# Rotated q and k channel-major by DMA, and the causal mask by VectorE, in a two-layer hybrid decoder trunk

## The chip, the cores and the metric

The kernel runs on one core of one Trainium2 chip. A core has engines that each work through their own queue of instructions in order: TensorE (PE, matrix products from SBUF into PSUM), VectorE (DVE), ScalarE (ACT), GpSimd (POOL) and SyncE (SP, here only a queue that issues DMAs). They wait for each other by semaphores. The metric is the device time of one execution in microseconds (us).

## The reference

Two layers over 512 tokens with 1024 channels; everything is float32. Each layer normalises x, projects it into ten groups of 512 columns, runs four mixers, gates each and projects back. Cut to what the change touches:

```python
x += W_out( concat_g[ mixer_g(RMSNorm(x)) * silu(gate_g) ] )    # g = A: S5, B: differential attention,
                                                                 #     C: RG-LRU, M: attention to 256 memory tokens
def rope_partial(x, cos, sin):          # q and k, the first 16 of the 64 channels of each half head
    x1, x2, xp = xf[..., :half], xf[..., half:ROPE_DIMS], xf[..., ROPE_DIMS:]
    out = jnp.concatenate([x1 * cos - x2 * sin, x2 * cos + x1 * sin, xp], axis=-1)

def diff_attention(q, k, v, lam):       # 4 heads, two softmaxes each
    mask = kpos[None, :] <= qpos[:, None]
    s1 = jnp.where(mask, s1, -1e30)     # s1 = q1 k1^T / 8, s2 likewise
    p = jax.nn.softmax(s1, axis=-1) - lam * jax.nn.softmax(s2, axis=-1)
```

## The kernel before

**Numbers.** A float32 product is made of three fp32r products: each operand is split into hi (rounded by ACT) and lo (the rest, by DVE), and PE sums hi x hi, hi x lo and lo x hi in PSUM.

**Weights.** All weights come in 136 pieces of 128x1024. `w_load` (L148) brings a piece into one of two raw buffers by a DMA of SP's queue; `w_use` splits it: ACT casts `whi` (L166), DVE subtracts `wlo` (L172). There are three buffers of each, so ACT and DVE can be about three pieces ahead of PE. A piece gives PE 24 products of 512 columns.

**Blocks.** `ORDER` (L31) lists the projection blocks of a layer: q, k, v, kv (the memory keys mk and values mv), cx (the RG-LRU's input), au (S5's input), the gates ag, bg, cg, mg, the memory query mq, S5's gl, and the output blocks o. `cm_block` (L504) keeps weights stationary and writes channel-major (channels on partitions, tokens along the row; products L517); `tm_block` (L524) keeps the tokens stationary and writes token-major (L537). Both take accumulators from a PSUM pool of four (`acc`). After every 12 products a block yields, which is one tick.

**Streams.** The mixers are generators that advance between ticks (`Streams`, L59; `run`, L1116): attention, RG-LRU (`lru`), S5 (`s5`), memory attention, parameter set-up (`par`). What a generator yields is the number of ticks until it goes on (`D_AT` = 2 for the attention). A scheduler of the framework then fixes the order of the instructions on each engine; at run time every engine keeps to that order.

**q and k.** Both are projected token-major. `qk_evac` (L574) copies a token tile by ACT into `qz`, rotates 16 of each 64 channels with four small DVE operations (`rab`, `qz`), and two ticks later `flush_qk` (L591) transposes it with four PE transposes (L597) into channel-major. For q ACT copies the result (L600); for k ACT casts one half (L605) and DVE subtracts for the other, which makes `kT`, hi and lo in the two halves of the partitions. The attention starts when q, k and v are there (L1272).

**Attention** (L610) works through 16 items (four query tiles of 128 by four heads). An item has a score tile `sc` of two softmaxes from a PSUM pool with one buffer. PE writes the scores (L647, L648), then adds the mask with a product of a bf16 identity and a bf16 mask, one for each softmax (L650). DVE takes the maximum (L652), ACT the exponentials with their sums (L658), DVE combines the two softmaxes (L664); then PE transposes (L672), ACT copies `pT`, PE multiplies with v (L682), ACT scales the result and squares it (L683, L685).

**RG-LRU** (L724) starts after cx: PE makes the gates' products (L740 to L742), ACT evaluates tanh, exponentials and a square root (L743 to L756), DVE scans over the tokens (L760). `lru_load` (L1126) brings its weights through GpSimd's DMA queue, up to `BD_AHEAD` blocks ahead of cx. **S5** (L927) rotates, scans and turns back blocks of 512 columns on DVE, and moves small `MT` tiles by GpSimd's queue.

## Time and profile before

| | us |
|---|---|
| median of 3 runs (913.62 to 914.91) | 913.9 |
| the profiled execution | 913.18 |
| its span, first to last instruction | 911.4 |
| PE busy | 890.5 |
| DVE busy | 658.8 |
| ACT busy | 509.6 |
| GpSimd busy | 42.1 |

Busy time counts the time in which at least one instruction of the engine is under way. Instructions of one engine overlap at their ends, so the mean length of one is a little more than the distance at which they follow each other. A wait is given with the instruction that ended last before it (`<-`). The granted clock of TensorE was 1.00 of full speed in all stretches.

### The profile page before, as it was taken

What the parts mean: (1) busy time and instruction counts of PE and PEld (TensorE: products, weight loads), DVE (VectorE), ACT (ScalarE), POOL (GpSimd) and SP (SyncE); (2) the same over time, 40 slices, a digit from 0 to 9 for tenths busy, and PEclk for the clock granted to TensorE, in tenths of its full rate; (3) what the DMA queues carried; (4) which work ended last, traced back from release to release, by engine and by line L of the source; (5) the groups of instructions that cost most, each with busy time, mean ns of one, the idle gap of its engine ahead of it and who ended that gap; (6) DMA issues with size and microseconds to landing.
All of it is one profiled execution on the core that took longest, in us unless ns stands there. A gap on an engine that the chain in (4) does not pass through costs nothing.

```text
span 911.4 us, 12490 instructions
## 1 busy us (share of the span) xinstructions
PE 890.5 (98%) x4542; PEld 748.9 (82%) x4542; DVE 658.8 (72%) x1315; ACT 509.6 (56%) x1031; POOL 42.1 (5%) x86
## 2 busy tenths in 40 slices
PE   8999999999999999999999999999999999999996
PEld 5788888978878888888888888898888888788885
DVE  6985888678999856983474667764899996666343
ACT  6764887985434265922554568766655344863133
POOL 1001000001110100000100000000101110000000
PEclk9999999999999999999999999999999999999999
DMA  5733432212222237432343332432112222152322
GB/s 185 196 118 102 140 93 70 70 47 72 75 70 61 75 104 205 135 111 93 127 140 92 93 93 70 137 95 70 51 47 83 63 74 93 47 185 98 108 72 93
DMA packets 80930, 90.07 MB, mean 99 GB/s; under 512 B 23778, under 2 KB 58211, under 8 KB 80868
## 3 DMA queue, kind: packets, MB, share of 16 engines
q1 hardware_dynamic: 77842, 85.72, 30.3%
q10 hardware_dynamic: 722, 2.36, 0.8%
q0 software_dynamic: 2304, 1.18, 0.5%
q8 instruction: 36, 0.59, 0.3%
q14 instruction: 26, 0.21, 0.1%
HBM read 84.40 MB, written 4.19 MB: 97 GB/s over the span
## 4 chain that ended last, share of the span: by engine, by line
PE 72%; DVE 18%; ACT 6%; issue 2%; DMA 1%; SPq 0%; DVEq 0%; ACTq 0%
PE acc L537 37%; PE acc L517 17%; PE acc L1261 5%; DVE wlo L172 2%; DVE u L347 2%; DVE xr L1046 2%; DVE wt L347 2%; PE ms L682 1%; DVE xr L347 1%; PE tp L312 1%; PE sc L810 1%; PE tp L1012 1%; PE sc L647 1%; PE sc L648 1%; ACT whi L166 1%
## 5 line engine op out<-in xcount | busy, mean ns | idle before, releaser
L172 DVE TENSOR_TENSOR wlo<-raw,whi 128x1024 fp32r<-128x1024 f32 x136 | 166.2, 1222 | 125.3 <-ACT whi L166 121.6
L166 ACT CAST whi<-raw 128x1024 fp32r<-128x1024 f32 x136 | 143.1, 1052 | 194.1 <-PE acc L537 120.1
L517 PE MATMUL acc<-hThi,whi 128*128 128x512 f32 x384 | 154.3, 402 | 0.0
L517 PE MATMUL acc<-hThi,wlo 128*128 128x512 f32 x384 | 151.1, 394 | 0.0
L517 PE MATMUL acc<-hTlo,whi 128*128 128x512 f32 x384 | 150.6, 392 | 0.0
L537 PE MATMUL acc<-whi,hThi 128*128 128x512 f32 x256 | 104.1, 407 | 1.0 <-ACT whi L166 1.0
L537 PE MATMUL acc<-wlo,hThi 128*128 128x512 f32 x256 | 100.7, 393 | 0.0
L537 PE MATMUL acc<-whi,hTlo 128*128 128x512 f32 x256 | 100.7, 394 | 0.0
L537 PE MATMUL acc<-wlo,mxh 128*128 128x512 f32 x256 | 100.2, 391 | 0.0
L537 PE MATMUL acc<-whi,mxh 128*128 128x512 f32 x256 | 100.1, 391 | 0.0
L537 PE MATMUL acc<-whi,mxl 128*128 128x512 f32 x256 | 100.1, 391 | 0.0
L517 PEld LDWEIGHTS acc<-hThi,wlo 128*128 128x128 f32 x384 | 72.2, 188 | 15.0
L517 PEld LDWEIGHTS acc<-hTlo,whi 128*128 128x128 f32 x384 | 72.4, 189 | 13.4
L517 PEld LDWEIGHTS acc<-hThi,whi 128*128 128x128 f32 x384 | 72.4, 189 | 13.0
L537 PEld LDWEIGHTS acc<-whi,hThi 128*128 128x128 f32 x256 | 56.3, 220 | 9.1 <-ACT whi L166 1.4
L537 PEld LDWEIGHTS acc<-whi,hTlo 128*128 128x128 f32 x256 | 56.1, 219 | 7.8 <-DVE hTlo L315 0.2
L537 PEld LDWEIGHTS acc<-wlo,hThi 128*128 128x128 f32 x256 | 56.4, 220 | 7.1
L537 PEld LDWEIGHTS acc<-whi,mxl 128*128 128x128 f32 x256 | 48.1, 188 | 9.8
L537 PEld LDWEIGHTS acc<-wlo,mxh 128*128 128x128 f32 x256 | 48.1, 188 | 9.7
L537 PEld LDWEIGHTS acc<-whi,mxh 128*128 128x128 f32 x256 | 48.1, 188 | 9.6
L982 POOL DMA_DIRECT2D MT<-kq x64 | 32.1, 509 | 490.7 <-DVE kq L347 339.4
L658 ACT ACTIVATE e<-sc,nmx 128x128 f32<-128x128 f32 (+3 forms) x64 | 33.1, 524 | 7.1 <-DVE nmx L654 5.8
(316 smaller groups left out, 1642.2 us busy)
## 6 DMA issues: line engine op xcount, KB each, us to landing
raw<-in_w_in_dram SPq DMA_DIRECT2D x80, 512.0 KB, 3.7
raw<-in_w_out_dram SPq DMA_DIRECT2D x32, 512.0 KB, 3.3
raw<-in_w_mem_kv_dram SPq DMA_DIRECT2D x16, 512.0 KB, 3.3
...
```

Of the source, the lines that this page charges most:

```text
L166: S.copy(hi, wbuf[j])
L172: V.tensor_tensor(out=lo, in0=raw, in1=hi, op=ALU.subtract)
L312: lastins["pe"] = PE.transpose(pt[:, k, :], h[:, kk * 128:(kk + 1) * 128], ident)
L347: V.tensor_tensor(out=o, in0=a, in1=b, op=op)
L517: PE.matmul(a[j][:, :ncol], w[:, kk, c], h(k), start=(hf == 0 and i == 0), stop=(hf == 1 and i == 3 * nh - 1))
L537: PE.matmul(a[t], h(k, t), w[:, kk, :], start=(p == 0 and kk == 0 and i == 0), stop=(p == np_ - 1 and kk == 1 and i == 2))
L647: PE.matmul(s[:, m, :M], qh[:, m, h, :], kT[m][:, h, :M], start=True, stop=False)
L648: PE.matmul(s[:, m, :M], ql[:, m, h, :], kT[m][:, h, :M], start=False, stop=False)
L658: S.activation(e[:, m, :N], s[:, m, :N], AF.Exp, bias=nmx[:, m:m + 1], scale=0.125, accum_out=sm[:, m:m + 1])
L982: G.dma_start(out=MT[g * 64 + 64 - n:g * 64 + 64, g, t], in_=kq[g * 64:g * 64 + n])
L1046: V.tensor_tensor_scan(out=xr_[i][:, j, :], data0=dec, data1=xr_[i][:, j, :], initial=0.0, op0=ALU.mult, op1=ALU.add)
L1261: PE.matmul(a, w[:, k, s, j * 128:(j + 1) * 128], h[:, 2 * hf + k, :], start=(hf == 0 and i == 0), stop=(hf == 1 and i == 5))
```

## The change

- q and k are projected channel-major by `cm_block`; ACT copies each 128x512 block straight into `z` (`qz`, `kz`). No PE transposes.
- `rope` collects the 32 + 32 + 32 + 32 rotated rows of `z` by four DMAs of GpSimd's queue into `rx`, DVE does four operations with tables of cosines and sines, and four DMAs bring the rows back. For k four ACT casts and four DVE subtracts of 64x1024 then make `kT`. `D_ROPE` gives the ticks between these steps.
- The tables are built once in channel-major form (GpSimd copies `rep`, eight PE transposes, four ACT copies), kept in DRAM, and loaded again in layer 1.
- The mask is float32 in SBUF (`cmt`), and DVE adds it to the score tile in PSUM before the maximum; the products of L650 and the bf16 tiles are gone.
- v comes first in both layers; the attention starts after k, as soon as the rope is done; `BD_AHEAD` is 1.

```diff
-ORDER = ["q v k kv cx au cg bg mq ag mg gl oAM0 oAM1 oBC0 oBC1".split(),
-         "q k cx v kv au mq bg mg ag cg gl oAM0 oAM1 oBC0 oBC1".split()]
+ORDER = ["v q k kv cx au cg bg mq ag mg gl oAM0 oAM1 oBC0 oBC1".split(),
+         "v q k cx kv au mq bg mg ag cg gl oAM0 oAM1 oBC0 oBC1".split()]
...
-BD_AHEAD = 3
+BD_AHEAD = 1
...
+D_ROPE = {"q": ((2, 2), (2, 2)), "k": ((4, 4), (2, 2))}
...
+    rtab = [b2([P, L], f"rt{i}") for i in range(2)]
+    rtd = [dpool.tile([P, L], F32, tag=f"rtd{i}", name=f"rtd{i}") for i in range(2)]
+    for w, src in enumerate((rcos, rsin)):
+        rep_ = b2([P, NT, P], "rep")
+        for i in range(NT):
+            G.tensor_copy(rep_[:, i].rearrange("p (a f c) -> p a f c", a=4, c=4),
+                          src[:, i].unsqueeze(1).unsqueeze(3).to_broadcast([P, 4, 8, 4]))
+        pr = tp()
+        for i in range(NT):
+            PE.transpose(pr[:, i, :], rep_[:, i], ident)
+        pf = pr.rearrange("p i c -> p (i c)")
+        for s_ in range(2):
+            S.activation(rtab[w][s_ * 64:s_ * 64 + 64], pf[s_ * 64:s_ * 64 + 64], AF.Copy, scale=-1.0 if w == 1 and s_ == 1 else 1.0)
+        G.dma_start(out=rtd[w], in_=rtab[w])
...
+    def rope(l, R, n):
+        z = R[n + "z"]
+        if l and n == "q":
+            rtab[:] = [b2([P, L], f"rt{i}") for i in range(2)]
+            for w in range(2):
+                G.dma_start(out=rtab[w], in_=rtd[w])
+        x1, x2 = b2([P, L], "rx"), b2([P, L], "ry")
+        rows = [(x1[s_ * 64 + m * 32:s_ * 64 + m * 32 + 32], z[m * 64 + s_ * 8:m * 64 + s_ * 8 + 8])
+                for s_ in range(2) for m in range(2)]
+        for x_, z_ in rows:
+            G.dma_start(out=x_, in_=z_)
+        yield D_ROPE[n][l][0]
+        co, si = rtab
+        for s_ in range(2):
+            to, fr = slice(s_ * 64, s_ * 64 + 64), slice(64 - s_ * 64, 128 - s_ * 64)
+            tt(x2[to], x1[fr], si[fr], ALU.mult)
+        tt(x1, x1, co, ALU.mult)
+        tt(x1, x1, x2, ALU.add)
+        for x_, z_ in rows:
+            G.dma_start(out=z_, in_=x_)
+        yield D_ROPE[n][l][1]
+        if n == "k":
+            kT = R["kT"] = [b8([P, 4, L], "kT", F32R) for _ in range(2)]
+            for h in range(0, 4, 2):
+                hs = slice(h, h + 2)
                 for m in range(2):
                     own, oth = slice(m * 64, m * 64 + 64), slice(64 - m * 64, 128 - m * 64)
-                    S.copy(dst[m][own, :, ts], pt[own])
-                    tt(dst[m][oth, :, ts], pt[own], dst[m][own, :, ts], ALU.subtract)
-
-    st.hook = flush_qk
+                    S.copy(kT[m][own, hs], z[own, hs])
+                    tt(kT[m][oth, hs], z[own, hs], kT[m][own, hs], ALU.subtract)
+                yield
 
     def attention(l, R):
-        while pend or "par" in st.live:
+        while any(n in st.live for n in ("par", "ropeq", "ropek")):
             yield
...
-                PE.matmul(s[:, m, :M], ql[:, m, h, :], kT[m][:, h, :M], start=False, stop=False)
-            for m in range(2):
-                PE.matmul(s[:, m, i * 128:N], idb, cmb, start=False, stop=True)
+                PE.matmul(s[:, m, :M], ql[:, m, h, :], kT[m][:, h, :M], start=False, stop=True)
+            tt(s[:, :, i * 128:N], s[:, :, i * 128:N], bc(cmt, 1, [P, 2, P]), ALU.add)
...
-            run(tm_block(h_tm(), qk_evac(R[n + "T"]), ids))
+            if u == 0:
+                R[n + "z"] = b8([P, 4, L], n + "z")
+            zt = R[n + "z"]
+
+            def z_evac(j, a, u=u, zt=zt):
+                S.copy(zt[:, 2 * u + j, :], a)
+            run(cm_block(h_cm(), 8, z_evac, ids))
+            if u == 1:
+                st.start("rope" + n, rope(l, R, n))
...
-        if n in ("q", "k", "v") and all(a in R for a in ("qT", "kT", "v")):
+        if n == "k" and u == 1:
             st.start("attn", attention(l, R))
```

The change moves instructions on every engine; three places follow. A row is line, operation, result<-operands, shape, and xN where alike instructions follow each other; numbers in names tell buffers apart, and the lines of the changed kernel differ (L517 is L534 there, L647/L648 are L662/L663, L172 is L175).

PE in layer 1, where the memory keys are projected. Before, an item's scores (`sc`) stand between the products of mk (`acc_5476`):

```order
L517 MATMUL acc_5476<-mhi_5172,wlo_5350 128x256
L517 MATMUL acc_5476<-mhi_5172,whi_5348 128x256
L647 MATMUL sc_5436<-kT_4754,qh_5372 128x256
L648 MATMUL sc_5436<-kT_4754,ql_5373 128x256
L647 MATMUL sc_5436<-kT_4755,qh_5372 128x256
L648 MATMUL sc_5436<-kT_4755,ql_5373 128x256
L650 LDWEIGHTS idb
L650 MATMUL sc_5436<-cmb,idb 128x128
L650 LDWEIGHTS idb
L650 MATMUL sc_5436<-cmb,idb 128x128
L517 MATMUL acc_5476<-mlo_5173,whi_5348 128x256
```

In the changed kernel four items stand one after the other, and only then comes the first product of the memory values mv (`acc_5497`); the last of the four items:

```order
L662 MATMUL sc_5587<-kT_5043,qh_5438 128x256
L663 MATMUL sc_5587<-kT_5043,ql_5439 128x256
L686 MATMUL tp_5606<-cst,e_5527 128x128 x2
L696 MATMUL ms_5611<-v_4512,pT_5539 128x128 x2
L662 MATMUL sc_5666<-kT_5042,qh_5438 128x256
L663 MATMUL sc_5666<-kT_5042,ql_5439 128x256
L662 MATMUL sc_5666<-kT_5043,qh_5438 128x256
L663 MATMUL sc_5666<-kT_5043,ql_5439 128x256
L686 MATMUL tp_5685<-cst,e_5597 128x128 x2
L696 MATMUL ms_5690<-v_4512,pT_5609 128x128 x2
L554 MATMUL acc_5497<-whi_5347,mhi_5066 128x512
```

There is no projection product between the scores any more.

ACT at the same place, where the RG-LRU ends (its square root is the 128x2048 row). Before, the weight casts `whi` and the copies of v stand between the square root and the first exponential:

```order
L756 ACT_TABLE_LOAD
L756 ACTIVATE li_5129<-li_5129 128x2048
L166 CAST whi_5302<-raw_5192 128x1024
L1171 COPY v_5105<-acc_5106 128x512
L1171 COPY v_5105<-acc_5107 128x512
L1171 COPY v_5105<-acc_5108 128x512
L1171 COPY v_5105<-acc_5109 128x512
L166 CAST whi_5348<-raw_5264 128x1024
L166 CAST whi_5414<-raw_5306 128x1024
L658 ACT_TABLE_LOAD
L658 ACTIVATE e_5392,sm_5393<-sc_5371,nmx_5390 128x128 x2
```

In the changed kernel the exponentials and the results of the attention (`e`, `pT`, `qz`, `jk`) alternate with the RG-LRU's functions (`a`, `lr`, `li`):

```order
L169 CAST whi_5499<-raw_5351 128x1024
L672 ACTIVATE e_5457,sm_5458<-sc_5437,nmx_5455 128x256 x2
L767 ACTIVATE a_1014_5494<-lr_5213 128x512
L765 ACTIVATE lr_5213<-lr_5213,cneg 128x512
L688 COPY pT_5539<-tp_5536 128x256
L697 ACTIVATE qz_4641<-ms_5541,rc_5379 128x128
L699 ACTIVATE jk_5544,oss_5106<-ms_5541,rc_5379 128x128
L767 ACTIVATE a_1031_5547<-lr_5213 128x512
L672 ACTIVATE e_5527,sm_5528<-sc_5517,nmx_5525 128x256 x2
L770 ACT_TABLE_LOAD
L770 ACTIVATE li_5214<-li_5214 128x2048
```

Attention and RG-LRU, one behind the other before, now share this part of ACT's queue.

DVE at the same place. Before, the first subtract of `kv`, which frees an accumulator of mk, stands among the scans `li` of the RG-LRU and the weight splits `wlo`:

```order
L654 TENSOR_SCALAR nmx_5390<-mx_5388 128x2
L347 TENSOR_TENSOR xc_4938<-xc_4938,li_5129 128x512
L172 TENSOR_TENSOR wlo_5416<-raw_5306,whi_5414 128x1024
L760 SCALAR_TENSOR_TENSOR li_5129<-lr_5128,xc_4938 128x512
L661 RECIPROCAL rc_5396<-sm_5393 128x2
L663 TENSOR_SCALAR cc_5398<-sm_5393,nlam,rc_5396 128x1
L347 TENSOR_TENSOR kv_5345<-acc_5346,kv_5344 128x256
L664 SCALAR_TENSOR_TENSOR e_5392<-e_5392,cc_5398 128x128
L652 TENSOR_REDUCE mx_5443<-sc_5436 128x2
L347 TENSOR_TENSOR kv_5345<-acc_5347,kv_5344 128x256
```

In the changed kernel all four scans and an item's mask add (`sc<-sc,cmt`), maximum and combine stand ahead of it:

```order
L352 TENSOR_TENSOR xc_4933<-xc_4933,li_5214 128x512 x2
L774 SCALAR_TENSOR_TENSOR li_5214<-lr_5213,xc_4933 128x512 x2
L352 TENSOR_TENSOR xc_4933<-xc_4933,li_5214 128x512 x2
L675 RECIPROCAL rc_5601<-sm_5598 128x2
L352 TENSOR_TENSOR sc_5666<-sc_5666,cmt 128x2x128
L677 TENSOR_SCALAR cc_5603<-sm_5598,nlam,rc_5601 128x1
L666 TENSOR_REDUCE mx_5672<-sc_5666 128x2
L678 SCALAR_TENSOR_TENSOR e_5597<-e_5597,cc_5603 128x256
L668 TENSOR_SCALAR nmx_5674<-mx_5672 128x2
L774 SCALAR_TENSOR_TENSOR li_5214<-lr_5213,xc_4933 128x512 x2
L352 TENSOR_TENSOR kv_5169<-acc_5170,kv_5168 128x256
```

The subtract has moved behind all of the RG-LRU's scans, and no weight split stands here.

DVE in layer 0, in the first block of S5 (`xr` are its rotated columns, the eight 128x128 rows its scans). Before, the scans stand in a row, with a weight split just ahead:

```order
L172 TENSOR_TENSOR wlo_2442<-raw_2283,whi_2440 128x1024
L347 TENSOR_TENSOR xr_489_2415<-xr_489_2415,u_2405 128x512
L1046 SCALAR_TENSOR_TENSOR xr_488_2414<-mag_280,xr_488_2414 128x128
L1046 SCALAR_TENSOR_TENSOR xr_489_2415<-mag_280,xr_489_2415 128x128
L1046 SCALAR_TENSOR_TENSOR xr_488_2414<-mag_280,xr_488_2414 128x128
L1046 SCALAR_TENSOR_TENSOR xr_489_2415<-mag_280,xr_489_2415 128x128
```

In the changed kernel an attention item's mask add, maximum and scaling stand among them:

```order
L352 TENSOR_TENSOR sc_2273<-sc_2273,cmt 128x2x128
L1057 SCALAR_TENSOR_TENSOR xr_435_2229<-mag_280,xr_435_2229 128x128
L666 TENSOR_REDUCE mx_2279<-sc_2273 128x2
L1057 SCALAR_TENSOR_TENSOR xr_436_2230<-mag_280,xr_436_2230 128x128
L668 TENSOR_SCALAR nmx_2281<-mx_2279 128x2
L1057 SCALAR_TENSOR_TENSOR xr_435_2229<-mag_280,xr_435_2229 128x128
```

The last items of layer 0's attention have moved into the S5 stage.

## Rows read from the trace of the kernel before

**Rows 1.** Page, part 1: busy us, share of the span, instructions.

```profile
PE 890.5 (98%) x4542; PEld 748.9 (82%) x4542; DVE 658.8 (72%) x1315; ACT 509.6 (56%) x1031; POOL 42.1 (5%) x86
```

**Rows 2.** Stretches: us, busy PE, PEld, DVE, ACT, POOL, PEclk, DMA share, GB/s.

```profile
200.00:300.00 100.00, 96.98 (x538) 82.29 (x537) 96.10 (x177) 44.45 (x96) 16.04 (x32) 1.00 0.22 67
535.00:550.00 15.00, 15.00 (x74) 12.18 (x73) 11.21 (x17) 14.07 (x23) 0.00 (x0) 1.00 0.22 70
550.00:600.00 50.00, 49.06 (x287) 43.07 (x287) 37.22 (x69) 38.05 (x86) 0.00 (x0) 1.00 0.38 116
```

**Rows 3.** Chain that ended last: start us, us, what, and how many instructions.

```profile
42.82 0.87 PE tp L597 x8
...
60.50 8.20 PE acc L537 x36
...
225.55 2.55 DVE xr L1046 x8
...
357.40 1.43 PE sc L810 x12
```

**Rows 4.** PE by line: xcount | busy us, mean ns | idle before.

```profile
L597 PE MATMUL tp<-cst,qz 128*128 128x128 f32 x64 | 8.9, 274 | 2.0 <-DVE tA L347 1.3 <-DVE kT L347 0.4 <-DVE rden L347 0.3
```

**Rows 5.** PE's instructions in time, a mask pair: start us, us.

```profile
573.89 0.29 PE L650 MATMUL sc<-cmb,idb 128*128 128x128 bf16 x2
573.98 0.36 PE L517 MATMUL acc<-mhi,whi 128*128 128x256 f32 x1
574.18 0.28 PE L517 MATMUL acc<-mlo,whi 128*128 128x256 f32 x1
```

**Rows 6.** DVE's instructions in time: the cosines' last operation.

```profile
30.06 0.19 DVE L393 TENSOR_SCALAR cs<-cs 128x64 f32<-128x64 f32 x1
```

**Rows 7.** GpSimd by line and shape, the fill nearest to a copy.

```profile
L499 POOL MEMSET WT<- 128x512 f32 x2 | 1.0, 524 | 0.3 <-POOLq L1361 0.3
```

**Rows 8.** GpSimd by line and shape, the issue of a 64 KB DMA.

```profile
L1133 POOL DMA_DIRECT2D bd<-in_lru_w_a_dram x4 | 2.6, 663 | 0.0
```

**Rows 9.** DMA issues: result<-operand, queue, count, KB each, median us to landing.

```profile
bd<-in_lru_w_x_dram POOLq DMA_DIRECT2D x4, 64.0 KB, 3.2
```

**Rows 10.** DVE by line and shape.

```profile
L172 DVE TENSOR_TENSOR wlo<-raw,whi 128x1024 fp32r<-128x1024 f32 x136 | 166.2, 1222 | 125.3 <-ACT whi L166 121.6 <-PE tp L828 3.0
...
L347 DVE TENSOR_TENSOR u<-tab,tab 128x512 f32<-128x512 f32 x16 | 11.0, 686 | 0.1
...
L652 DVE TENSOR_REDUCE mx<-sc 128x2 f32<-128x1024 f32 x8 | 9.8, 1221 | 2.1 <-PE sc L650 2.1
L760 DVE TENSOR_TENSOR_SCAN li<-lr,xc 128x512 f32<-128x512 f32 x8 | 9.6, 1212 | 0.0
```

**Rows 11.** ACT by line and shape.

```profile
L166 ACT CAST whi<-raw 128x1024 fp32r<-128x1024 f32 x136 | 143.1, 1052 | 194.1 <-PE acc L537 120.1 <-PE acc L517 52.9 <-issue 10.8
...
L658 ACT ACTIVATION_READ_ACCUMULATOR e<-sc,nmx 128x1 f32 x64 | 12.7, 199 | 0.0
L683 ACT ACTIVATE qT<-ms,rc 128x128 f32<-128x128 f32 x32 | 11.9, 371 | 5.6 <-PE ms L682 5.3
...
L631 ACT CAST qh<-qT 64x512 fp32r<-64x512 f32 x16 | 9.9, 619 | 0.2
...
L658 ACT ACTIVATE e<-sc,nmx 128x256 f32<-128x256 f32 x16 | 7.4, 471 | 1.1 <-DVE nmx L654 1.1
...
L743 ACT ACTIVATE lr<-tp,hb 128x512 f32<-128x512 f32 x8 | 5.5, 686 | 0.0
```

**Rows 12.** ACT's instructions in time, near layer 0's square root.

```profile
190.59 0.38 ACT L685 ACTIVATE jk<-ms,rc 128x128 f32<-128x128 f32 x1
190.84 0.22 ACT L685 ACTIVATION_READ_ACCUMULATOR jk<-ms,rc 128x1 f32 x1
...
193.04 1.28 ACT L756 ACT_TABLE_LOAD   x1
...
194.33 1.92 ACT L756 ACTIVATE li<-li 128x2048 f32<-128x2048 f32 x1
```

More of the change, by code (lines that the diff above doesn't have):

```diff
@@ L11 @@
 F32R = mybir.dt.float32r
-BF16 = mybir.dt.bfloat16
 I32 = mybir.dt.int32
@@ L101, in tile_kernel, with bc @@
     ps = ctx.enter_context(tc.tile_pool(name="ps", bufs=1, space=bass.MemoryType.PSUM))
+    def bc(ap, axis, shape):
+        return ap.unsqueeze(axis).to_broadcast(shape)
     uid = [0]
@@ L182, in tile_kernel @@
     xr = A["x"].rearrange("o (t p) d -> p (o t) d", p=P)
-    xd = ctx.enter_context(tc.tile_pool(name="xd", bufs=1, space=bass.MemoryType.DRAM)).tile([L, D], F32, tag="xd", name="xd")
+    dpool = ctx.enter_context(tc.tile_pool(name="xd", bufs=1, space=bass.MemoryType.DRAM))
+    xd = dpool.tile([L, D], F32, tag="xd", name="xd")
     xdr = xd.rearrange("(t p) d -> p t d", p=P)
@@ L234, in tile_kernel @@
                 add(l, "o", n[1:], ps_)
-            elif n in ("q", "k", "v", "au"):
+            elif n in ("v", "au"):
                 add(l, n, 0, tm_pieces(w_in[l], COL[n]))
@@ L259, in tile_kernel @@
     nc.sync.dma_start(out=posi, in_=A["positions"].rearrange("o (t p) -> p (o t)", p=P))
-    cmk = b2([P, P], "cmk")
-    nc.sync.dma_start(out=cmk, in_=A["consts"][:, C_CM:C_CM + 128])
+    cmt = const.tile([P, P], F32, tag="cmt", name="cmt")
+    nc.sync.dma_start(out=cmt, in_=A["consts"][:, C_CM:C_CM + 128])
     vec = b2([P, DEPTH, P], "vec")
@@ L484, in params @@
         V.tensor_scalar(out=cpos, in0=cpos, scalar1=4.0, scalar2=None, op0=ALU.mult)
-    idb = const.tile([P, P], BF16, tag="idb", name="idb")
-    cmb = const.tile([P, P], BF16, tag="cmb", name="cmb")
-    V.tensor_copy(idb, ident)
-    V.tensor_copy(cmb, cmk)
+    rtab = [b2([P, L], f"rt{i}") for i in range(2)]
[12 more added lines that the diff above has]
+        G.dma_start(out=rtd[w], in_=rtab[w])
     nsum = const.tile([P, NT], F32, tag="nsum", name="nsum")
@@ L571, in h_au @@
         return ((lambda k, t: hi[k // 4][:, k % 4, t, :]), (lambda k, t: lo[k // 4][:, k % 4, t, :]))
-    def qk_evac(dst):
-        def f(t, a):
-            z = b2([P, 8, 64], "qz")
-            S.copy(z, a.rearrange("p (m d) -> p m d", d=64))
-            z12 = z[:, :, 0:16].rearrange("p m (s f) -> p m s f", f=8)
-            ca = rcos[:, t, :].unsqueeze(1).unsqueeze(1).to_broadcast([P, 8, 2, 8])
-            sa = rsin[:, t, :].unsqueeze(1).unsqueeze(1).to_broadcast([P, 8, 2, 8])
-            rab = b2([P, 2, 8, 2, 8], "rab")
-            ra, rb = rab[:, 0], rab[:, 1]
-            tt(ra, z12, ca, ALU.mult)
-            tt(rb, z12, sa, ALU.mult)
-            tt(z12[:, :, 0, :], ra[:, :, 0, :], rb[:, :, 1, :], ALU.subtract)
-            tt(z12[:, :, 1, :], ra[:, :, 1, :], rb[:, :, 0, :], ALU.add)
-            pend.append((dst, t, z, st.now))
-        return f
@@ L590, in tile_kernel @@
-    pend = []
-    def flush_qk():
-        while pend and st.now - pend[0][3] >= 2:
-            dst, t, z, _ = pend.pop(0)
-            pt = tp()
-            for j in range(4):
-                PE.transpose(pt[:, j, :], z[:, 2 * j:2 * j + 2, :].rearrange("p m d -> p (m d)"), ident)
-            ts = slice(t * 128, (t + 1) * 128)
-            if len(dst) == 1:
-                S.copy(dst[0][:, :, ts], pt)
-            else:
+    def rope(l, R, n):
[23 more added lines that the diff above has]
+                hs = slice(h, h + 2)
@@ L612, in attention @@
             yield
-        qT, kT, v = R["qT"][0], R["kT"], R["v"]
+        qT, kT, v = R["qz"], R["kT"], R["v"]
         o = qT
@@ L856, in tile_kernel @@
     tab1 = const.tile([P, 2, 16, 8], F32, tag="tab1", name="tab1")
-    def bc(ap, axis, shape):
-        return ap.unsqueeze(axis).to_broadcast(shape)
     def s5_params(l, R):
@@ L1164, in tile_kernel @@
         if n in ("q", "k"):
-            R[n + "T"] = [b8([P, 4, L], "qT")] if n == "q" else [b8([P, 4, L], "kT", F32R) for _ in range(2)]
-            run(tm_block(h_tm(), qk_evac(R[n + "T"]), ids))
+            if u == 0:
[6 more added lines that the diff above has]
+                st.start("rope" + n, rope(l, R, n))
         elif n == "v":
```

## The prediction

> **What bounds the kernel now.** I read the page's shares first: TensorE (PE) is busy 98% of the span, VectorE (DVE) 72%, ScalarE (ACT) 56% [rows 1]. So an average cannot say what the change is worth; the stretches can [rows 2]. While layer 0's S5 mixer runs (200 to 300 us) DVE is busy 96.10 of 100 us and PE already loses 3.02. Where layer 1's RG-LRU runs (535 to 550 us) ACT is busy 14.07 of 15 us, and PE loses nothing; with the attention behind it (550 to 600 us) PE loses 0.94. The chain of waits gives PE's pace [rows 3]: 0.228 us for a matmul of 512 columns (36 in 8.20 us), 0.12 for 256 columns (12 in 1.43 us), 0.11 for a transpose (8 in 0.87 us). Everywhere else PE runs without gaps, so work taken off it counts, as long as ACT and DVE deliver the split weights in time. That is the question here, because the change moves the two heaviest users of ACT and DVE to another place.
>
> **Work taken off PE, and put on.** The 64 transposes of q and k go: eight groups of 8 at 0.87 us [rows 3] are 7.0 us, and the 2.0 us that PE waited ahead of them [rows 4] go too. The 64 mask products go: a pair starts 0.09 us ahead of the next instruction, and the fp32r product behind it takes 0.20 us where its kind takes 0.12 [rows 5]. 17 of the 32 pairs stand ahead of such a product, 15 ahead of a transpose (0.13 us by the row of that kind): 17 x 0.17 + 15 x 0.13 = 4.8 us. Eight new transposes for the rope tables cost 0.9 us. They stand inside v's third weight piece, which PE reaches near 30 us; the cosines are there at 30.25 us [rows 6], and four GpSimd copies of 128x128 come between. No such copy is in the trace; the nearest row, a fill of 128x512, takes 0.524 us [rows 7], so four take 0.5 us (by elements) to 2.1 us. PE waits for them, 0.5 to 2.7 us; I take 2.2, nearer the whole fill, since a copy also reads. Sum on PE: -7.0 - 2.0 - 4.8 + 0.9 + 2.2 = **-10.7 us** (ends -8 and -13).
>
> TensorE transposes are dear by the Trainium skill ("TensorE: Matmul & The Clock Gate", Part 4: about 275 ns each in a kernel's context). By that figure the 64 would be worth an estimated 17.6 us; the chain's 0.87 us for 8 says 7.0, since they overlap, and the measurement decides.
>
> **The moved rows.** Rope now needs four DMAs of 64 KB out, four DVE operations, four DMAs back, all from GpSimd's queue. The RG-LRU's loads have the same size and queue: 0.663 us to issue, 3.2 us to land [rows 8, 9]. Four issues and a landing are 4 x 0.663 + 3.2 = 5.9 us each way, with the four DVE operations (0.686 each, [rows 10]) 14.5 us in all. Behind k stand cx's two column blocks in layer 1, 96 products or 21.9 us, ahead of the first scores; in layer 0 more. I cost these DMAs at nothing; if the cover were gone, each us beyond 21.9 is one us of PE.
>
> **The layer-1 stage (the largest term).** Before, the attention started after v, when the RG-LRU had nearly finished. Now v comes first, and attention and RG-LRU both start after cx, in front of the memory keys mk, whose products have only 256 columns: 96 of them, 11.5 us for four weight pieces that still cost ACT and DVE a full split each. The order shows it: on PE the scores of attention items 4 to 7 stand back to back ahead of `acc_5497`, and ACT has the gates, the exponentials and the casts in one row.
> From the end of cx to `acc_5497`, PE has 96 x 0.12 + 32 scores x 0.12 + 24 gate products x 0.228 + about 27 transposes and small products x 0.11 = **23.8 us** of work.
> ACT, in its order from `cx_5162` to the square root, has: 8 casts of 1024 columns (four weight pieces, four kT halves) x 1.052 = 8.4; 20 gate functions of 512 columns x 0.686 = 13.7; the square root 1.92 and two table loads x 1.28 = 4.5; 8 exponentials of 128 columns (0.371, by the row of another function of that size) and 4 of 256 (0.471), each with an accumulator read (0.199), = 7.2; 4 pairs of scaled copies and squares = 3.8; 14 casts and copies of 512 columns x 0.62 = 8.7; 9 small copies x 0.37 = 3.3 [rows 11, 12]. That is 49.6 us for 90 instructions; in a packed stretch the next one starts about 0.1 us before the last ends (0.25 us after the start of a 0.38 us one), except behind table loads and SBUF casts [rows 12], so 75 x 0.1 comes off: **42.1 us**.
> Behind the square root DVE still has, in order, two updates, two scans, two updates, the mask add, maximum and combine of an item, two scans and only then the subtract of `kv` that frees the accumulator `acc_5497` needs: 4 x 0.686 + 4 x 1.212 + about 2.5 for seven small ones (halves and quarters of the 512-column rows) [rows 10], less 13 x 0.1, = 8.8 us.
> So PE gets `acc_5497` at 42.1 + 8.8 = 50.9 us where its own work ends at 23.8: it stands for **27 us**. The weights behind it are then ready and add nothing. Less the 0.94 us lost there before: **+26** (ends 18, if another 0.1 us of overlap an instruction is hidden, and 35, if none is).
>
> The Trainium skill ("ScalarE: Activation LUTs", What ACT_TABLE_LOAD costs) puts a drain of about 1.38 us beside each 1.28 us load. The trace shows none: the load at 193.04 us is followed by its function 1.29 us later [rows 12]. By the page's figure an estimated 2.8 us would be added to the term for two loads.
>
> **The layer-0 S5 stage.** The attention of layer 0 follows k in both kernels, but now waits for k's rope (4 and 4 ticks by `D_ROPE`, a tick being 12 products or 2.7 us), some 20 us, so its last four items now run among the first two S5 blocks. The order shows mask adds, maxima and combines between the turns and scans there. From the first rotated block (`sc_2203`) to the weight split `wlo_2635` DVE has 44 operations of 512 columns x 0.605 (0.686 less the overlap), 16 short scans x 0.32 (8 in 2.55 us), 3 splits x 1.14, 3 maxima x 1.12, 11 operations of 256 columns x 0.36 and about 2 us of small ones: 26.6 + 5.1 + 3.4 + 3.4 + 4.0 + 2.0 = 44.5 us [rows 3, 10]. PE's work over the same rows is 107 + 12 products x 0.228 + 72 small ones x 0.1 = 34.3 us. DVE is 10 us late. Of that, PE lost 3.0 us before already [rows 2]; I take **+6** (ends 0 and 10). The mask adds are 3 of the 11; alone they are 1.1 us, so it is the overlap of the two stages that costs.
>
> Sum against the profiled execution's 913.2 us (0.7 us under the median): 913.2 - 10.7 + 26 + 6 = **934.5 us**.
>
> **Rivals.**
> (a) *PE stays the bound*: ACT and DVE run ahead, since before shows ACT at 94% of a stretch with PE unharmed [rows 2]; then only PE's sum counts: 913.2 - 10.7 = 902.5 us, faster. It decides if PE's work from cx to `acc_5497` is over about 45 us, which the order does not give. By the Trainium skill ("Perfetto Trace Analysis", Optimization Strategy and the section ahead of it) one shortens the engine with the highest occupancy; that is PE, and the page would give this rival; the same page says that the regime can change over time, and the stretches agree.
> (b) *Half of it*: DVE's subtract is not what PE waits for, and layer 0 costs nothing: ACT alone up to the next exponential pair, 42.1 + 2.6 = 44.7, less the 23.8, less the low end's 7 us of further overlap: +14; 913.2 - 10.7 + 14 = 916.5 us, and up to 925 with a part of layer 0.
> (c) *The rope comes late*: GpSimd's queue holds q's and k's row moves, the table reload and the RG-LRU loads in one row. If each leg takes twice 5.9 us, the way is 26 us, 4 us over the cover in layer 1, and the ACT queue behind the kT casts moves with it: 938 to 950 us.
>
> **How the numbers follow.** Forecast (925 to 943 us) 0.66; (b) 0.16; (a) and what lies between it and no change (902 to 912 us) 0.12; (c) and more (above 943) 0.04; within 0.2% (about what a measurement of this kernel can tell from no change) 0.02. The range 915 to 943 holds the forecast and (b), 0.82. Faster 0.12, same 0.02, slower 0.86.
>
> **What would show it.** Right: PE idle by some 20 us or more between the last cx product and the first product of `mv` (`acc_5497`), about 510 to 560 us, released by DVE's kv subtract or ACT; ACT and DVE near full in that stretch; PE idle of several us near 215 to 250 us, released by DVE; DMA waits nowhere. PE's busy time down by some 12 us. Wrong: a PE share still at 98%, ACT instructions packed far below the sums above, or the rope's DMAs as releaser of PE or ACT.

## The result and the profile after

| | before | changed |
|---|---|---|
| median, us (4 runs each, 912.57 to 914.91 and 945.48 to 949.83) | 913.76 | 947.82 |
| ratio, with its 95% interval | | 1.0368 (1.0348 to 1.0387) |
| the profiled execution, its span | 913.18, 911.4 | 947.35, 945.6 |

The changed kernel is 3.7% slower. The direction was forecast, the size was not: from profiled execution to profiled execution it lost 34.2 us where the sum said 21.3, and 947.8 us lies above the range (915 to 943). The changed kernel's page, part 1 (busy us, share, instructions) and two rows of part 2 (tenths in 40 slices; PEclk is the granted clock):

```profile
PE 894.6 (95%) x4422; PEld 749.4 (79%) x4422; DVE 665.3 (70%) x1289; ACT 507.0 (54%) x1019; POOL 64.8 (7%) x130
...
PE   7999899999999999999999969399999999999997
...
PEclk9999999999999999999999989589999999999999
```

PE has 120 instructions fewer than in [rows 1] and is busy 4 us longer: less work, some of it at a lower clock. PE is short in slices 24 and 26 (544 to 567 and 591 to 615 us), and the clock in 24, 26 and 27. By stretches (columns as in [rows 2]):

```profile
200.00:300.00 100.00, 97.17 (x547) 80.34 (x547) 96.96 (x194) 55.63 (x133) 12.07 (x24) 1.00 0.19 56
550.00:600.00 50.00, 33.69 (x190) 28.85 (x188) 35.23 (x62) 37.77 (x78) 0.00 (x0) 0.85 0.21 65
600.00:625.00 25.00, 14.43 (x49) 11.51 (x50) 20.56 (x41) 16.28 (x39) 0.00 (x0) 0.55 0.08 22
```

The S5 stretch of layer 0 is as full as before. From 550 us on PE is busy 33.69 of 50 us where [rows 2] has 49.06, then 14.43 of 25 us at a granted clock of 0.55. PE's instructions in time that stood still there (start, us, instruction, in brackets the idle time ahead and what ended it):

```profile
561.26 0.58 PE L662 MATMUL sc<-kT,qh 128*128 128x256 f32 x1 [4.94 <-DVE kT L352]
564.43 0.58 PE L662 MATMUL sc<-kT,qh 128*128 128x256 f32 x1 [2.37 <-DVE kT L352]
566.38 1.94 PE L317 MATMUL tp<-cst,mt 128*128 128x128 f32 x8 [1.16 <-DVE mlo L320]
...
594.58 0.38 PE L662 MATMUL sc<-kT,qh 128*128 128x256 f32 x1 [3.47 <-ACT qh L647]
...
600.83 0.58 PE L662 MATMUL sc<-kT,qh 128*128 128x256 f32 x1 [3.04 <-ACT e L672]
...
611.48 0.58 PE L662 MATMUL sc<-kT,qh 128*128 128x256 f32 x1 [2.92 <-ACT e L672]
615.57 0.66 PE L686 MATMUL tp<-cst,e 128*128 128x128 f32 x2 [2.86 <-DVE nmx L668]
618.26 0.79 PE L554 MATMUL acc<-whi,mhi 128*128 128x512 f32 x1 [1.17 <-DVE kv L352]
```

The last row is the prediction's `acc_5497`, and DVE's `kv` subtract does end its wait. But the waits begin 57 us ahead of it, at the first scores.

**A ledger.** To compare kernels I add up, over PE's instructions in time, how much later each next one starts than the pace of [rows 3] allows (0.228 us for 512 columns, 0.12 for 256, 0.11 for a transpose, and about that for a mask product), and call it *loss*. It holds idle time and half clock alike. Before has 31.7 us of it, the changed kernel 79.4, and 13.5 us less of paced work (some 7 us of them mask products).

| stretch, us | loss before | changed |
|---|---|---|
| 0 to 100 | 11.0 | 10.3 |
| 100 to 150 (layer 0: k's end, kv) | 1.5 | 8.0 |
| 150 to 200 | 0.9 | 3.5 |
| 200 to 300 (S5, layer 0) | 5.7 | 8.3 |
| 550 to 575 (cx's end, first scores) | 0.8 | 12.2 |
| 575 to 625 (mk, up to mv) | 2.5 | 27.6 |
| the rest | 9.3 | 9.5 |

### The profile page after: what moved, and what is told of

The parts are those of the page before. It is cut to its first block, busy times and chain, and to the rows that moved or that the text cites. A ratio compares the mean times of both kernels' runs of the same rounds, so it can differ in the third digit from the quotient of the medians.

```text
span 945.6 us, 12259 instructions
## 1 busy us (share of the span) xinstructions
PE 894.6 (95%) x4422; PEld 749.4 (79%) x4422; DVE 665.3 (70%) x1289; ACT 507.0 (54%) x1019; POOL 64.8 (7%) x130
## 4 chain that ended last, share of the span: by engine, by line
PE 66%; DVE 20%; ACT 9%; DMA 2%; issue 2%; POOL 0%; SPq 0%; DVEq 0%; ACTq 0%
PE acc L554 27%; PE acc L534 25%; PE acc L1279 5%; DVE wlo L175 3%; DVE u L352 2%; DVE xr L1057 2%; DVE wt L352 2%; ACT whi L169 1%; PE tp L317 1%; DVE xr L352 1%; PE sc L824 1%; DVE mx L666 1%; PE tp L1023 1%; DVE li L774 1%; PE tp L849 1%
## 5 line engine op out<-in xcount | busy, mean ns | idle before, releaser
L175 DVE TENSOR_TENSOR wlo<-raw,whi 128x1024 fp32r<-128x1024 f32 x136 | 166.2, 1222 | 146.9 <-ACT whi L169 138.9
L534 PE MATMUL acc<-hThi,whi 128*128 128x512 f32 x512 | 203.3, 397 | 0.0
L534 PE MATMUL acc<-hThi,wlo 128*128 128x512 f32 x512 | 202.1, 395 | 0.5 <-DVE wlo L175 0.5
L534 PE MATMUL acc<-hTlo,whi 128*128 128x512 f32 x512 | 201.7, 394 | 0.0
L534 PEld LDWEIGHTS acc<-hThi,wlo 128*128 128x128 f32 x512 | 96.5, 189 | 20.1 <-DVE wlo L175 0.7
L534 PEld LDWEIGHTS acc<-hTlo,whi 128*128 128x128 f32 x512 | 96.8, 189 | 18.5
L534 PEld LDWEIGHTS acc<-hThi,whi 128*128 128x128 f32 x512 | 96.8, 189 | 18.5 <-DVE bg L734 0.2
L554 PE MATMUL acc<-whi,hThi 128*128 128x512 f32 x128 | 53.6, 419 | 2.1 <-ACT whi L169 2.1
L554 PE MATMUL acc<-wlo,hThi 128*128 128x512 f32 x128 | 51.3, 401 | 0.0
L554 PE MATMUL acc<-whi,hTlo 128*128 128x512 f32 x128 | 50.8, 400 | 0.0
L662 PE MATMUL sc<-kT,qh 128*128 128x256 f32 (+2 forms) x64 | 23.3, 370 | 22.3 <-DVE kT L352 10.4
L554 PEld LDWEIGHTS acc<-whi,hThi 128*128 128x128 f32 x128 | 32.2, 252 | 5.4 <-ACT whi L169 2.5
L662 PEld LDWEIGHTS sc<-kT,qh 128*128 128x128 f32 x64 | 13.1, 205 | 27.7 <-DVE kT L352 11.5
```

The costliest lines, as they stand in the source:

```text
L175: V.tensor_tensor(out=lo, in0=raw, in1=hi, op=ALU.subtract)
L534: PE.matmul(a[j][:, :ncol], w[:, kk, c], h(k), start=(hf == 0 and i == 0), stop=(hf == 1 and i == 3 * nh - 1))
L554: PE.matmul(a[t], h(k, t), w[:, kk, :], start=(p == 0 and kk == 0 and i == 0), stop=(p == np_ - 1 and kk == 1 and i == 2))
L662: PE.matmul(s[:, m, :M], qh[:, m, h, :], kT[m][:, h, :M], start=True, stop=False)
```

## The experiments

Each kernel is the changed one with one idea put in, but for `e8_mask_only`, which starts from the kernel before. Ratios are to the kernel before, run beside it on the same chip. The edits are cut to their core (`...`, and set-up lines of the mask left out), and where only a `+` line stands it replaces the line of the same name.

**The mask alone.** Before, with the mask added by DVE and nothing else:

```diff
-                PE.matmul(s[:, m, :M], ql[:, m, h, :], kT[m][:, h, :M], start=False, stop=False)
-            for m in range(2):
-                PE.matmul(s[:, m, i * 128:N], idb, cmb, start=False, stop=True)
+                PE.matmul(s[:, m, :M], ql[:, m, h, :], kT[m][:, h, :M], start=False, stop=True)
+            tt(s[:, :, i * 128:N], s[:, :, i * 128:N], cmt.unsqueeze(1).to_broadcast([P, 2, P]), ALU.add)
```

> The kernel before with one part of the change alone: the mask is added by DVE. By PE's account: 64 products less, 4.8 us less, 908 to 910 us. By the rival that DVE's 32 adds of 0.42 us lengthen each item behind the one score buffer and push DVE further over PE in the S5 stretches: 914 to 920 us.

910.17 us, ratio 0.9957 (0.9943 to 0.9972), and it is the fastest kernel of this study. PE's busy time falls by 3.8 us against [rows 1], DVE's rises by 8.4, and the kernel gains all the same. Page part 1, and DVE by line and shape, of this kernel:

```profile
PE 886.7 (98%) x4478; PEld 745.8 (82%) x4478; DVE 667.2 (73%) x1345; ACT 510.9 (56%) x1032; POOL 42.3 (5%) x86
```
```profile
L347 DVE TENSOR_TENSOR sc<-sc,cmt 128x256 f32<-128x256 f32 x32 | 13.7, 427 | 10.4 <-PE sc L644 9.5 <-ACT jk L680 0.9
```

**The mask given back to PE** in the changed kernel:

```diff
+                PE.matmul(s[:, m, :M], ql[:, m, h, :], kT[m][:, h, :M], start=False, stop=False)
+            for m in range(2):
+                PE.matmul(s[:, m, i * 128:N], idb, cmb, start=False, stop=True)
-            tt(s[:, :, i * 128:N], s[:, :, i * 128:N], bc(cmt, 1, [P, 2, P]), ALU.add)
```

> The changed kernel with the mask added by PE again (64 bf16 products), the DVE adds gone. Collision theory: PE's 4.8 us come back where PE is the bound, and DVE's 13 us leave a stage that ACT bounds: 946 to 953. Mask theory: 15 us or more less, under 933.

950.58 us, 1.0392 (1.0376 to 1.0407). The loss from 550 to 625 us stays (39.1 us). The mask is not what made the stage slow. It does matter in the S5 stretch of layer 0: with the mask on PE, PE is busy 99.58 of 100 us there, where the changed kernel has 97.17 (columns as in [rows 2]):

```profile
200.00:300.00 100.00, 99.58 (x571) 83.14 (x570) 96.38 (x189) 56.37 (x134) 12.07 (x24) 1.00 0.18 57
```

**Layer 1 in the old order**, with the attention started when q, k and v are all there:

```diff
-         "v q k cx kv au mq bg mg ag cg gl oAM0 oAM1 oBC0 oBC1".split()]
+         "q k cx v kv au mq bg mg ag cg gl oAM0 oAM1 oBC0 oBC1".split()]
...
-        if n == "k" and u == 1:
+        if (n == "k" and u == 1 or n == "v") and all(a in R for a in ("qz", "kz", "v")):
```

> The changed kernel with layer 1's blocks in the order of before (q k cx v kv) and the attention started when q, k and v are there; everything else stays changed. Collision theory (attention and RG-LRU side by side in front of the memory keys cost the 36 us): 908 to 915 us, no PE wait over 2 us behind cx, granted clock 1.00 from 500 to 650 us. Mask theory (32 mask adds by DVE lengthen every item, the one score buffer makes PE wait): it stays above 935. Rope theory (the rotated rows and kT come late): it stays above 930, since kT is made as late as before.

922.55 us, 1.008 (1.0063 to 1.0097). The stage's loss falls from 39.8 to 7.4 us: the order is the cause. But it misses the expected time, because a new loss of 9.5 us stands at 450 to 500 us. PE's waits in that stretch (us in total, times, longest):

```profile
PE tp L317 <- DVE h L307: 5.5, 2, 3.5
```

q is now the layer's first block, and a channel-major product has all 512 tokens along its row: PE needs every normalised token before it can begin, where the token-major q began with the first 128. Putting v first had been hiding this.

**The RG-LRU moved away**: in layer 1 it starts after mv, the attention stays.

```diff
-            if u == 1:
+            if u == 1 and l == 0:
                 st.start("lru", lru(l, R))
...
+        if n == "mv" and l == 1:
+            st.start("lru", lru(l, R))
```

> The changed kernel with one thing moved: in layer 1 the RG-LRU starts after mv, not after cx. The blocks, the rope, the attention and their place stay. Collision theory (ACT's sum of attention plus RG-LRU, and DVE's scans ahead of the kv subtract, hold mk): of the 36 us lost between 550 and 625 us under 15 remain, those at the front behind kT; the RG-LRU gives some back in the blocks behind: 918 to 932 us. Rival (attention beside mk's short products is too much by itself, with the mask on DVE and one score buffer): 25 us or more remain there, 938 or more.

926.06 us, 1.0134 (1.0118 to 1.0149): 22 us of the 34 come back. Its stretches:

```profile
550.00:575.00 25.00, 16.49 (x94) 14.22 (x93) 19.10 (x32) 13.86 (x25) 0.00 (x0) 0.80 0.19 62
575.00:600.00 25.00, 24.53 (x143) 20.79 (x143) 20.29 (x43) 19.09 (x53) 0.00 (x0) 1.00 0.46 147
600.00:625.00 25.00, 25.00 (x119) 23.48 (x119) 18.72 (x36) 22.77 (x53) 0.00 (x0) 1.00 0.20 64
```

Attention beside mk costs next to nothing; the front, 550 to 575 us, is as bad as ever (11.6 us). So there are two causes, one of which this edit doesn't touch.

**The attention moved away**, as a mirror of that run, and **delayed by four ticks**:

```diff
-        if n == "k" and u == 1:
+        if (n == "k" and u == 1 and l == 0) or (n == "mk" and u == 1 and l == 1):
```
```diff
+        if l == 1:
+            yield 4
```

> The changed kernel, only that layer 1's attention starts after the memory keys mk, not after k; the RG-LRU starts after cx as before. It is the mirror of the run that moved the RG-LRU. Theory (attention and RG-LRU together ahead of mk's short products are what costs, and the first scores' wait for kT adds some 11 us): the RG-LRU alone stands beside mk, kT is long ready, so the loss of TensorE between 550 and 625 us falls from 39.8 us to below 15, as it did when the RG-LRU was moved (15.1), and without that run's waits for kT. Attention then reaches further into S5 (650 to 725 us), where up to 12 us may be lost anew: 920 to 935 us. Rival (it is the short products of mk with the RG-LRU that cost, whatever the attention does): at least 30 us stay between 550 and 625 us, 940 us or more.

> The changed kernel, only that layer 1's attention begins 4 ticks (of 12 products) later, with the RG-LRU where it was. It parts the front (first scores that wait for kT behind cx's casts and subtracts) from the collision of the two mixers. Theory (two causes added: a front of about 11 us and a collision of about 25 us): the waits for kT go, the loss between 550 and 575 us falls by 5 to 11 us, the collision stays: 937 to 943 us. Rival 1 (one cause, the sum of ACT's and DVE's work up to the first mv product sets the end whatever PE does at the front): the loss moves but keeps its size, 945 to 950 us. Rival 2 (it is only where the attention starts that costs): the loss falls below 20 us, under 932 us.

957.01 us, 1.0459 (1.0442 to 1.0477), and 942.56 us, 1.0306 (1.0291 to 1.0322). Neither removed the front: in both, the framework's scheduler still put the first item's scores ahead of mk on PE, and PE still waited for `kT` (5.42 and 2.38 us in each). So `e12` didn't test what it was made for, and that its time lies in the range expected without the front (937 to 943) is luck. What the two did change is the number of attention items in the stretch, and with `e9` that makes a series:

| | items, 550 to 625 us | RG-LRU there | loss 550 to 575 | loss 575 to 625 |
|---|---|---|---|---|
| changed | 8 | yes | 12.2 | 27.6 |
| e12 | 5.5 | yes | 12.6 | 22.8 |
| e11 | 3 | yes | 12.6 | 18.4 |
| e9 | 10 | no | 11.6 | 3.5 |

Every item costs 1.8 to 1.9 us beside the RG-LRU. Carried on to no item, the line leaves 18.4 - 3 x 1.85 = 12.9 us for the RG-LRU by itself (an estimate: no kernel ran without items, and the items are not all of one size). So my expectation for `e11`, below 15 us, failed, and its rival (30 us or more between 550 and 625 us) had the better of it: the RG-LRU beside mk's short products costs already alone. The waits in `e11` show it, PE in time:

```profile
593.19 0.58 PE L662 MATMUL sc<-kT,qh 128*128 128x256 f32 x1 [4.11 <-ACT e L672]
...
605.57 0.80 PE L554 MATMUL acc<-whi,mhi 128*128 128x512 f32 x1 [1.95 <-DVE kv L352]
```

and the stretch from 575 us (columns as in [rows 2]):

```profile
575.00:600.00 25.00, 16.73 (x109) 15.11 (x108) 15.59 (x23) 23.57 (x39) 0.00 (x0) 0.82 0.26 85
```

ACT is busy 23.57 of 25 us with the RG-LRU's functions and mk's own casts, and one exponential queued behind them holds PE. `e11` is slower than the changed kernel in all, since its attention then reaches into S5, where 16.3 us more are lost between 700 and 750 us (loss 18.7 there, 2.5 in the changed kernel).

**cx ahead of q and k** in layer 1; the same with `BD_AHEAD` 3; and the same with ag between k and kv in layer 0:

```diff
+         "v cx q k kv au mq bg mg ag cg gl oAM0 oAM1 oBC0 oBC1".split()]
```
```diff
+         "v cx q k kv au mq bg mg ag cg gl oAM0 oAM1 oBC0 oBC1".split()]
...
+BD_AHEAD = 3
```
```diff
+ORDER = ["v q k ag kv cx au cg bg mq mg gl oAM0 oAM1 oBC0 oBC1".split(),
+         "v cx q k kv au mq bg mg ag cg gl oAM0 oAM1 oBC0 oBC1".split()]
```

> The changed kernel with layer 1's blocks in the order v cx q k kv: v stays first, the RG-LRU runs beside the wide blocks q and k, the attention beside kv. Collision theory (layer 1's 36 us come from attention and RG-LRU sharing ACT's queue in front of mk, and the 9 us that the order of before then lost come from q being first and needing all of the normalised tokens): both go, 909 to 916 us, granted clock 1.00 from 500 to 650 us. If instead the channel-major q and k or the rope make layer 1 slow wherever they stand: 920 or more.

> As e5_cx_first, with the RG-LRU's weights loaded three blocks ahead of cx as before, not one, so that they do not share the DMA engines with mk's weights. If these loads hold up mk's weights in layer 0 (ACT waited 9.6 us for them): 2 to 5 us less than e5_cx_first. If mk's weights are late by themselves: within 1 us of it.

> As e5_cx_first, and in layer 0 the gate block ag stands between k and kv, so k's rope is over when mk begins and the attention runs beside it. If layer 0's 6.5 us near 113 us come from mk and mv running ahead of their weight DMAs with nothing beside them: 4 to 8 us less than e5_cx_first. If they come from the rope's and the RG-LRU's DMAs in the way of the weights: no gain, since all of these DMAs are still there.

933.8 us, 1.0216 (1.02 to 1.0232); 933.15 us, 1.0211 (1.0197 to 1.0226); 944.03 us, 1.0329 (1.0314 to 1.0343). `e5` does empty the stage (loss 8.9 us), but misses the expected time: 16.6 us are lost at 675 to 725 us, where the changed kernel lost 1.8. PE's waits of `e5` from 670 to 730 us:

```profile
PE sc L662 <- ACT e L672: 4.3, 2, 4.0
PE sc L662 <- DVE u L352: 3.2, 1, 3.2
```

The attention starts later there, so its last and longest items stand among S5's DVE work. `e7` is the same within the intervals, so the RG-LRU's loads are no cause. `e6` was for layer 0. The loss at 100 to 125 us, 7.0 in the changed kernel, is 0.7 in it, but its attention too is pushed into S5 and loses 18.0 us between 175 and 225 us (2.9 in the changed kernel).

**The rope's waits shortened**, in layer 1, and in layer 0:

```diff
+D_ROPE = {"q": ((2, 2), (2, 2)), "k": ((4, 4), (1, 1))}
```
```diff
+D_ROPE = {"q": ((2, 2), (2, 2)), "k": ((2, 2), (2, 2))}
```

> The changed kernel with the two waits of layer 1's k rope at 1 and 1 ticks, not 2 and 2. If the front of the stage is held by kT (PE waited 4.94 and 2.37 us for DVE's kT subtract, 1.16 for mlo, at half clock behind that): 8 to 11 us less, 937 to 940. If kT only waits in ACT's and DVE's order and what comes behind is the bound: under 3 us less, 945 to 948.

> The changed kernel with the two waits of layer 0's k rope at 2 and 2 ticks, not 4 and 2. If layer 0's loss (about 6.5 us near 113 us, PE 3.04 us behind DVE's kT subtract and then at half clock) comes from where kT's casts fall among the memory values' evacuations: 3 to 7 us less, 941 to 945. If it comes from the weight DMAs, which landed late there: no change within 1.5 us.

947.85 us, 1.0367 (1.0352 to 1.0383), and 950.45 us, 1.0387 (1.0371 to 1.0402). Neither gained. In `e2` the rows go back 1.9 us earlier (545.67 us, 547.57 in the changed kernel), but ACT's casts for `kT` begin at 557.88 us, 558.28 before the edit: they stand behind a weight cast that starts at 556.93. The first two waits for `kT` shrink to 3.46 and 1.59 us, and 4.58 us for an exponential follow at once, so the loss from 550 to 575 us is 14.6 us, not smaller. In `e4` the first casts begin at 113.69 us, 113.28 before the edit. It is the place in ACT's and DVE's queues that holds `kT`, not the DMAs of the rope; what a `kT` ready much earlier would be worth wasn't tried.

**q as before, k channel-major**, old orders, mask by DVE (the edit cut to its core; `qk_evac` and `flush_qk` are those of before):

```diff
-ORDER = ["v q k kv cx au cg bg mq ag mg gl oAM0 oAM1 oBC0 oBC1".split(),
-         "v q k cx kv au mq bg mg ag cg gl oAM0 oAM1 oBC0 oBC1".split()]
+ORDER = ["q k v kv cx au cg bg mq ag mg gl oAM0 oAM1 oBC0 oBC1".split(),
+         "q k cx v kv au mq bg mg ag cg gl oAM0 oAM1 oBC0 oBC1".split()]
...
-            elif n in ("v", "au"):
+            elif n in ("q", "v", "au"):
```

> The parts of the change that the account finds good, in the order of before: the mask by DVE; k channel-major with its rotated rows moved by DMA behind v (layer 0, order q k v) and behind cx and v (layer 1, order of before); q token-major with its transposes as before; the attention after v as before. If rope by DMA costs nothing where a wide block stands behind it: 32 transposes less (3.5 us and their part of the waits) and the mask's 4 us: 904 to 908 us. If the kT casts of 1024 columns or the row moves cost PE even there: 909 to 914.

917.59 us, 1.0034 (1.0022 to 1.0046), a miss: with wide blocks behind k, and with the RG-LRU and attention one behind the other again, it is still 7 us behind `e8`. Its loss is 5.0 us at 25 to 50 us (2.5 in `e8`) and 9.2 at 550 to 600 us (3.1). The largest single wait at 20 to 50 us:

```profile
PE acc L534 <- ACT qz L594: 3.3, 1, 3.3
```

Half of the transposes are saved (3.5 us by the prediction's price), and more than that is paid at k's blocks. Which part of that is the channel-major form and which the mixers' new places, these runs don't tell.

## Why the prediction was right, and where it was wrong

**PE's account: right in its parts, too small by the ledger.** 13.5 us of paced work went, 10.7 forecast, a little past the far end (13). The ledger's pace makes some 7 us of the mask products, where 4.8 were forecast; measured alone, in `e8`, the mask is worth 3.9 us (914.1 x 0.0043). For `rep` PE waited 0.8 us, not 2.2 (PE's waits from 20 to 50 us, changed kernel):

```profile
PE tp L502 <- POOL rep L498: 0.8, 1, 0.8
```

**The rows moved by DMA: right that PE doesn't wait for them, wrong that the step costs nothing.** k's issues leave at 534.58 us and the way back is issued at 547.57, 13.0 us later; GpSimd in time, of the changed kernel:

```profile
534.58 2.19 POOL L603 DMA_DIRECT2D rx<-kz  x4 [6.69 <-ACT kz L1181]
547.57 2.28 POOL L612 DMA_DIRECT2D kz<-rx  x4 [10.79 <-DVE rx L352]
```

Four issues take 2.2 us, 0.55 each, where I used 0.663. PE and ACT never waited for these DMAs, but DVE did, three times (at 70, 94 and 520 us), for 13.3 us in all; its waits in the changed kernel:

```profile
DVE ry L352 <- DMA rx<-qz: 10.9, 2, 6.0
...
DVE ry L352 <- DMA rx<-kz: 2.4, 1, 2.4
```

The step that failed is "in layer 0 more [cover]. I cost these DMAs at nothing". PE has cover for the DMAs, but attention, which starts behind them, no longer stands among the products of mk, and PE runs through mk's four weight pieces faster than they come. A piece is 96/4 products of 256 columns, 2.9 us at PE's pace, and lands 3.4 us after its issue. ACT's waits from 80 to 122 us (us, times, longest), and the page's row of that DMA (count, KB, us to landing), changed kernel:

```profile
ACT whi L169 <- DMA raw<-in_w_mem_kv_dram: 9.6, 4, 3.4
...
ACT whi L169 <- DMA raw<-in_w_in_dram: 4.0, 2, 3.1
```

```profile
raw<-in_w_mem_kv_dram SPq DMA_DIRECT2D x16, 512.0 KB, 3.4
```

In the kernel before ACT waited 0.6 us for weights there, and the prediction's sign "DMA waits nowhere" failed. The casts of `kT` queue behind those late `whi`, and PE's scores behind them (3.04 us at 116.06). Price: 6.5 us between 100 and 150 us. `e6` supports this: with ag's wide products between k and mk one of those waits was left (2.4 us), and 0.7 us of loss from 100 to 125. `e4` shows that the rope's ticks don't move it.

**The layer-1 stage: right mechanism, term mis-sized (+26 forecast, +36.5 measured, past the far end of 35).** Both of its sums came out. From the end of cx to the end of the square root ACT was busy 42.8 us (42.1 forecast), and from there to the `kv` subtract DVE took 8.65 (8.8). ACT and DVE in time:

```profile
557.13 0.58 ACT L1199 COPY cx<-acc 128x512 f32<-128x512 f32 x1
...
558.28 3.99 ACT L621 CAST kT<-kz 64x1024 fp32r<-64x1024 f32 x4
...
567.50 0.58 ACT L319 CAST mhi<-tp 128x512 fp32r<-128x512 f32 x1 [4.13 <-PE tp L317]
...
605.89 1.28 ACT L770 ACT_TABLE_LOAD   x1
607.19 1.91 ACT L770 ACTIVATE li<-li 128x2048 f32<-128x2048 f32 x1
```
```profile
609.13 1.29 DVE L352 TENSOR_TENSOR xc<-xc,li 128x512 f32<-128x512 f32 x2 [0.57 <-ACT li L770]
...
617.78 1.09 DVE L352 TENSOR_TENSOR kv<-acc,kv 128x256 fp32r<-128x256 f32 x3
```

The failed step is the one that let ACT run from the end of cx without a gap: "So PE gets `acc_5497` at 42.1 + 8.8 = 50.9 us". It took 62 (556.3, where PE's last cx product ends, to 618.26). From 557.13 to 609.10 ACT had 9.2 us of gaps; the rest of the 11.1 us is 0.8 ahead of ACT's first copy, 0.5 more in the two sums, and 0.5 from the subtract's start to the product. The largest gap, 4.13 us, comes from DVE; its instructions in time:

```profile
554.94 2.32 DVE L1205 SCALAR_TENSOR_TENSOR xc<-cx,pv,xc 128x509 f32<-128x509 f32 x3 [2.84 <-ACT xc L1203]
557.26 1.23 DVE L175 TENSOR_TENSOR wlo<-raw,whi 128x1024 fp32r<-128x1024 f32 x1
558.42 1.53 DVE L1205 SCALAR_TENSOR_TENSOR xc<-cx,pv,xc 128x509 f32<-128x509 f32 x2
559.99 2.35 DVE L352 TENSOR_TENSOR kT<-kz,kT 64x1024 fp32r<-64x1024 f32 x2
562.37 0.75 DVE L1205 SCALAR_TENSOR_TENSOR xc<-cx,pv,xc 128x511 f32<-128x511 f32 x1
563.15 2.36 DVE L352 TENSOR_TENSOR kT<-kz,kT 64x1024 fp32r<-64x1024 f32 x2
565.54 1.29 DVE L320 TENSOR_TENSOR mlo<-tp,mhi 128x512 fp32r<-128x512 f32 x2
```

ACT waits there for the second half of the transposes of the memory tokens (`mt`). These need one of the two `tp` buffers, and PE's row at 566.38 has DVE's `mlo` subtract as what freed it. `mlo` stands behind cx's updates, a weight split and the four subtracts of `kT`, and DVE has no gap over 0.15 us from 554.94 us until past it. The prediction added up ACT's row up to the square root, and DVE's only behind it; at the front it is DVE that is full. The first scores stand ahead of those transposes on PE, but they end near 565.2 us, so they are not what the transposes waited for. All runs with k, cx and kv in a row keep a loss of 11.6 to 14.6 us there; `e1` and `e5`, which change that order, are rid of it. No run moved DVE's work alone.

One forecast came out by luck: between the last cx product and `acc_5497` PE stood idle for 26.9 us by the profile, 27 forecast, but its busy time there was 35.06 us, not 23.8, since products at half clock and products that stand alone are longer. The stretch (columns as in [rows 2]):

```profile
556.32:618.26 61.94, 35.06 (x188) 29.93 (x187) 47.77 (x89) 48.82 (x109) 0.00 (x0) 0.73 0.14 43
```

The clock has a part in this, and the prediction left it out although it foresaw 27 us of idle PE. After the wait of 4.94 us the granted clock is 0.50 (the 1.2 GHz level), and the eight transposes at 566.38 take 1.94 us, 0.87 in [rows 3]; it is back at 1.00 by 572 us. It falls again at 596 and returns about 622 us. Products of 256 columns follow each other in 0.21 us there, 0.12 otherwise. At the stage's two edges that makes about 4.6 us: 1.07 for the transposes (inside ACT's gap of 4.13), 15 x 0.09 for mk's first products, and 0.9 + 1.3 for mv's first ones (1.74 us at half rate to 620, and 10 us at a mean of 0.87). Between the edges PE mostly waits, and what the slow scores add there stays open. The Trainium skill ("TensorE: Matmul & The Clock Gate", HAM oscillation) says that gaps in PE's work bring the half rate back, which is paid on top of the wait; these rows agree, and the loss column above holds both.

**What of the stage is what.** Of the 36.5 us, 11.4 are the front. 25.1 are the collision (27.6 less 2.5), and by the series about half of that is the RG-LRU beside short products, half the attention items in the same queue (by themselves the items cost almost nothing, as `e9` shows). That is sharper than the prediction's "attention and RG-LRU both start after cx". It is also less certain, since the split rests on a line through three points.

**The S5 stage of layer 0: too high.** +6 forecast, +2.6 measured, inside its ends. DVE is at 96.96 of 100 us, as before. The prediction has "it is the overlap of the two stages that costs" and the mask adds at 1.1 us; `e3` speaks against that, since with the adds off DVE, and the overlap kept, PE loses 0.42 us of the 100, less than the 3.02 before (the mask products put back there fill about 1 us of it, an estimate: eight at 0.11). Which of DVE's instructions hold PE there, no run parts further.

**The sum again**, with what the ledger gives: -13.5 + 36.5 + 6.5 (100 to 150) + 2.6 (150 to 200) + 2.6 (S5) - 0.5 (the rest) = +34.2. The error of 12.9 us is 10.5 from layer 1's stage and 9.1 in layer 0 for which nothing had been set down, less 3.4 and 2.8 that S5 and PE's work came out better; the rest is 0.5.

**The rivals.** (a), 902.5 us, and (b), 916 to 925, fell: PE had no work to cover ACT with. (a) stood on the page that would shorten the busiest engine ("Perfetto Trace Analysis" in the Trainium skill); PE's work did go, and only `e8`, where nothing else moved, turned it into time. (c), the rope late, gave the right time (938 to 950) for another reason: only DVE waited for the rope's DMAs, its waits lie outside the stage, and `e2` with half the ticks for layer 1's k changed nothing. The table loads are as forecast: the square root starts 1.30 us after its load, without a drain.
